# A hybrid RWKV-7 and RG-LRU layer on one core: both roundings of a weight tile ahead of both subtractions

## The chip, the cores and the metric

The kernel runs on one core of a Trainium2 chip. A core has five engines that work side by side, each through its own queue in order: TensorE (PE in the profile; its weight loads are the row PEld), VectorE (DVE), ScalarE (ACT), GpSimd (POOL) and SyncE (SP), which here only issues transfers. The metric is the device time of one execution in microseconds. An engine that reaches an instruction whose input isn't there waits, and everything behind it in its queue waits too.

## The reference, cut to what matters

One layer of a decoder takes 1024 tokens of a prompt and 8 sequences of 4 new tokens, 1056 columns together, each of 1024 channels, all in fp32:

```python
z = x @ w_in                                  # 1024 -> 3*1024+256 RWKV, 2*1024 LRU, 2*1024 gates
yA, S = _rwkv7_branch(z[..., :RWKV_COLS], ...)   # token shift, low-rank decay/gate, wkv state
yB, new_conv, h_last = _rglru_branch(xb, gb, ...)  # conv of 4, gated linear recurrence
merged = sigmoid(ga) * yA + sigmoid(gb2) * yB
h1 = layer_norm(ALPHA * x + merged @ w_o)
y  = layer_norm(ALPHA * h1 + (silu(h1 @ w_ffn_gate) * (h1 @ w_ffn_up)) @ w_ffn_down)
```

The RWKV branch is, for each head of 64 channels, a state S (64 x 64) that each token decays, corrects by a rank-one term and extends by another:

```python
sa = einsum('bhij,bhj->bhi', S, -kk_t)
S = S * w_t + sa * (kk_t * a_t) + v_t * k_t
y_t = einsum('bhij,bhj->bhi', S, r_t)
```

## The kernel before, in words

**Products in three parts.** TensorE multiplies in a rounded fp32 format. To keep the precision, each factor is split into a rounded part and the rest (x into xh and xl, a weight tile into wh and wl), and each product is three matmuls: wh with xh, wh with xl, wl with xh.

**Stages.** First the projection w_in: 58 tiles of 128 output columns, each for two halves of the tokens (one of them in two pieces of 300 and 256 columns, the other in one of 512). A list, STREAM, sets the order in which these tiles come. Eight *units* (half p of the tokens, pair of head groups) of the RWKV branch run beside it as background tasks: the preparation of the operands (rge, kta, arm, rb, bk), the inverse of a triangular block (btmp and bt on VectorE, then bounced through a buffer in memory, scrZ, to zt and tdv), a chain of eight chunks (xs, su), and the gating, whose result mgd goes to memory. The LRU branch and the sample tokens are background tasks too. Then follow the output projection w_o (16 tiles, split again from mgd), the layer norm, the feed-forward part in five splits of its hidden tiles (the long plain stretch of the profile), and the second layer norm.

**Who sets the order.** All instructions go through a `Ticker`, a list scheduler that works while the program is written. Each task is a generator that queues its instructions; only the first pending one of each task is a candidate. The ticker issues the candidate that can start first by its own table of costs, and between equals the one of the task with the smaller priority number. So within a task the order is fixed; between tasks it is decided by these costs. Main-program instructions are recorded at line 246, all instructions of background tasks at line 316, so that nearly all the units' work has the one line L316, and the names of tiles tell it apart.

**Weights.** The class `Weights` runs a task of priority 0 that brings the weight tiles, in order of use, through two raw buffers (wraw, 512 KB each transfer, issued by GpSimd's queue) and two pairs of split buffers (wh, wl). For tile j it waits until tile j − 2 is in use no more, then treats the two halves of the tile (PARTS = 2; `k` holds four of eight blocks of 128 x 128 each): `A` is ScalarE's copy with rounding into wh, `TT` VectorE's subtraction raw − wh into wl. From tile 132 on (N_IN; behind the projection's and LRU's tiles) the second half's subtraction is `PTT`, the same on GpSimd. Then the tile counts as arrived, and the transfer of tile j + 2 is issued into the raw buffer.

Of the kernel before, what the change touches and what calls it, by code (L numbers as in the profile page):

```python
# [345 lines left out]
def tile_hybrid_step(ctx: ExitStack, tc: tile.TileContext, I, O):  # L346
# [16 lines left out]
    def A(out, in_, func=AF.Copy, scale=1.0, bias=0.0):  # L363
        return act.activation(out, in_, func, bias=bias, scale=scale)
# [47 lines left out]
    class Weights:  # L412
# [21 lines left out]
        def split(self):  # L434
            for j, (_, nk) in enumerate(self.srcs):
                while not self.rest if j >= len(self.srcs) - 8 else self.used + len(self.h) <= j:
                    yield
                raw, (h, l) = self.raw[j % len(self.raw)], self.parts(j)
                for part in range(self.PARTS):
                    k = slice(part * nk // self.PARTS, (part + 1) * nk // self.PARTS)  # L440
                    A(h[:, k], raw[:, k])
                    (PTT if part in ON_POOL and j >= N_IN else TT)(l[:, k], raw[:, k], h[:, k].bitcast(F32), OP.subtract)
                tk.later(self.arrived)
                if j + len(self.raw) < len(self.srcs):
                    self.load(j + len(self.raw))
# [32 lines left out]
    with ExitStack() as zctx:  # L478
# [1097 lines left out]
        def merged_first():  # L1576
            for k in range(8):
                split(early[k % 4], k, 544, "mA")
                if k < 4:
                    load_cols(early[k], mgd[k + 4], cols)  # L1580
            yield
# [9 lines left out]
        def merged_last():  # L1591
            t = yield from temps.take()
            stage = [t, pp, vzs[0][:, 0], vzs[0][:, 1]]
            for k in range(8):
                while (6, "fin") not in F or k > 5 and (7, "fin") not in F:
                    yield
                load_cols(stage[k % 4], mgd[k], ((512, 1024),))
                if k > 2:
                    split(stage[(k - 3) % 4], k - 3, 512, "mB")
                if k == 5:  # L1600
                    for x in (3, 4, 5):
                        split(stage[x % 4], x, 512, "mB")
            for x in (6, 7):
                split(stage[x % 4], x, 512, "mB")
# [356 lines left out]
```

## Time and profile before

| | |
|---|---|
| time, median of 3 runs | 2149.74 us |
| the three runs | 2144.78, 2149.74, 2162.22 us |
| the profiled execution, its own time | 2161.04 us |
| its span in the trace | 2159.3 us |
| mean granted clock of TensorE in it | 0.965 |
| TensorE busy | 2057.3 us, 95% |
| VectorE busy | 1239.0 us, 57% |
| ScalarE busy | 1072.5 us, 50% |
| GpSimd busy | 395.7 us, 18% |
| VectorE's subtractions into wl | 344, 263.2 us |
| ScalarE's roundings into wh | 424, 250.7 us |

The profiled execution took 11.3 us longer than the median. Durations and waits come from its trace; a forecast from them is put on the median by its difference. A row of a group gives line, engine, operation, out<-in, the count, busy time and mean, and then the engine's idle time just ahead of these instructions with what ended most of it. A row of the timeline gives start, duration and, in brackets, the idle time ahead with its releaser.

### The profile page before, as it was taken

What the parts mean: (1) busy time and instruction counts of PE and PEld (TensorE: products, weight loads), DVE (VectorE), ACT (ScalarE), POOL (GpSimd) and SP (SyncE); (2) the same over time, 40 slices, a digit from 0 to 9 for tenths busy, and PEclk for the clock granted to TensorE, in tenths of its full rate; (3) what the DMA queues carried; (4) which work ended last, traced back from release to release, by engine and by line L of the source; (5) the groups of instructions that cost most, each with busy time, mean ns of one, the idle gap of its engine ahead of it and who ended that gap; (6) DMA issues with size and microseconds to landing.
All of it is one profiled execution on the core that took longest, in us unless ns stands there. A gap on an engine that the chain in (4) does not pass through costs nothing.

```text
span 2159.3 us, 44129 instructions
## 1 busy us (share of the span) xinstructions
PE 2057.3 (95%) x17664; PEld 1782.9 (83%) x17664; DVE 1239.0 (57%) x2999; ACT 1072.5 (50%) x2491; POOL 395.7 (18%) x813
## 2 busy tenths in 40 slices
PE   7799999989989999999999899999999999999996
PEld 7788888988987777777777697889999999999986
DVE  5576786786777786877867656522322323223227
ACT  4656665757657768676676736821121121121221
POOL 1101211211311310202112020211211111112124
PEclk9899997999999999999989799999999999999998
DMA  4131231231232231222313423211111111112112
GB/s 136 56 97 40 73 102 35 67 87 60 90 112 65 77 94 50 81 72 78 89 45 95 132 96 119 98 55 37 56 49 31 58 45 35 59 35 65 39 40 81
DMA packets 125565, 152.85 MB, mean 71 GB/s; under 512 B 82912, under 2 KB 87424, under 8 KB 125360
## 3 DMA queue, kind: packets, MB, share of 16 engines
q0 software_dynamic: 32576, 112.75, 15.6%
q1 hardware_dynamic: 92784, 37.28, 7.0%
q8 instruction: 139, 2.28, 0.4%
q14 instruction: 66, 0.54, 0.1%
HBM read 132.45 MB, written 17.57 MB: 69 GB/s over the span
## 4 chain that ended last, share of the span: by engine, by line
PE 74%; DVE 11%; ACT 9%; issue 3%; DMA 1%; POOL 1%; POOLq 0%; SPq 0%; DVEq 0%; ACTq 0%
PE bank L246 60%; PE bank L316 15%; DVE tmp L316 2%; ACT tmp L316 2%; DVE wl L316 1%; ACT wh L316 1%; DVE su L316 1%; ACT L316 1%; ACT nz L316 1%; DVE btmp L316 1%; ACT arm L316 1%; DVE bt L316 1%; ACT bk L316 1%; DVE arm L316 1%; DVE rge L316 1%
## 5 line engine op out<-in xcount | busy, mean ns | idle before, releaser
L246 PE MATMUL bank<-xx,wh 128*128 128x512 f32 (+4 forms) x3168 | 801.0, 340 | 28.6 <-ACT xx L246 9.1
L246 PEld LDWEIGHTS bank<-xx,wh 128*128 128x128 f32 x3168 | 547.3, 194 | 89.8 <-ACT xx L246 9.0
L246 PE MATMUL bank<-xx,wl 128*128 128x512 f32 (+4 forms) x1584 | 537.1, 339 | 0.0
L316 DVE TENSOR_TENSOR wl<-wraw,wh 128x512 fp32r<-128x512 f32 (+1 forms) x344 | 263.2, 767 | 265.3 <-ACT wh L316 260.8
L316 ACT ACTIVATE wh<-wraw 128x512 fp32r<-128x512 f32 (+2 forms) x424 | 250.7, 599 | 287.1 <-PE bank L246 248.0
L246 PE MATMUL bank<-hl,wh 128*128 128x272 f32 (+1 forms) x1056 | 342.4, 324 | 0.9 <-DVE hl L316 0.9
L246 PE MATMUL bank<-hh,wh 128*128 128x272 f32 (+1 forms) x1056 | 341.0, 323 | 0.5 <-ACT hh L316 0.5
L246 PE MATMUL bank<-hh,wl 128*128 128x272 f32 (+1 forms) x1056 | 341.3, 323 | 0.0
L246 PEld LDWEIGHTS bank<-xx,wl 128*128 128x128 f32 x1584 | 307.2, 194 | 28.2 <-issue 3.0
L246 PEld LDWEIGHTS bank<-hh,wh 128*128 128x128 f32 x1056 | 198.6, 188 | 17.3 <-ACT hh L316 1.2
L246 PEld LDWEIGHTS bank<-hl,wh 128*128 128x128 f32 x1056 | 198.6, 188 | 17.2 <-DVE hl L316 1.5
L246 PEld LDWEIGHTS bank<-hh,wl 128*128 128x128 f32 x1056 | 198.5, 188 | 15.4
L316 POOL DMA_DIRECT2D wraw<-in_win x114 | 61.9, 543 | 778.4 <-DVE wl L316 480.7
L246 PE MATMUL bank<-u,wh 128*128 128x272 f32 (+1 forms) x864 | 197.5, 322 | 0.0
L316 POOL TENSOR_TENSOR wl<-wraw,wh 128x512 fp32r<-128x512 f32 (+2 forms) x80 | 90.5, 1131 | 525.6 <-ACT wh L316 502.8
L246 PEld LDWEIGHTS bank<-u,wh 128*128 128x128 f32 x864 | 143.9, 188 | 12.9
L316 DVE TENSOR_TENSOR acc<-acc,bank 128x272 f32<-128x272 f32 (+3 forms) x120 | 62.2, 519 | 140.7 <-PE bank L246 138.9
L246 PE MATMUL bank<-u,wl 128*128 128x272 f32 (+1 forms) x432 | 139.4, 323 | 0.0
L316 ACT ACTIVATE sg<-bank 128x272 f32<-128x272 f32 (+1 forms) x66 | 30.8, 466 | 195.8 <-PE bank L246 195.8
L316 DVE TENSOR_TENSOR sg<-sg,bank 128x272 f32<-128x272 f32 (+1 forms) x66 | 34.4, 521 | 157.5 <-PE bank L246 157.4
L316 ACT ACTIVATE u<-sg 128x272 fp32r<-128x272 f32 (+1 forms) x66 | 33.1, 502 | 114.2 <-DVE sg L316 114.2
L316 ACT ACTIVATE su<-bank 64x256 f32<-64x256 f32 (+1 forms) x192 | 60.2, 337 | 59.3 <-PE bank L316 57.0
(248 smaller groups left out, 3154.5 us busy)
## 6 DMA issues: line engine op xcount, KB each, us to landing
wraw<-in_win POOLq DMA_DIRECT2D x116, 512.0 KB, 3.6
wraw<-in_wgu POOLq DMA_DIRECT2D x48, 512.0 KB, 3.5
wraw<-in_wo POOLq DMA_DIRECT2D x16, 512.0 KB, 3.6
wraw<-in_wdn POOLq DMA_DIRECT2D x24, 256.0 KB, 2.9
wraw<-in_wdn POOLq DMA_DIRECT2D x16, 320.0 KB, 3.1
mgd<-yb POOLq DMA_DIRECT2D x32, 128.0 KB, 2.6
out_y<-tmp SPq DMA_DIRECT2D x8, 512.0 KB
scrN<-nz SPq DMA_DIRECT2D x64, 32.0 KB
```

Of the source, the lines that this page charges most:

```text
L246: fn(*args, **kw)
L316: fn(*args, **kw)
```

## The change

Within a weight tile's task the two halves are no longer treated one after the other (rounding, subtraction, rounding, subtraction), but the two roundings are queued first and then the two subtractions. Number, size and engine of the instructions stay.

```diff
-                for part in range(self.PARTS):
-                    k = slice(part * nk // self.PARTS, (part + 1) * nk // self.PARTS)
+                ks = [slice(part * nk // self.PARTS, (part + 1) * nk // self.PARTS) for part in range(self.PARTS)]
+                for k in ks:
                     A(h[:, k], raw[:, k])
+                for part, k in enumerate(ks):
                     (PTT if part in ON_POOL and j >= N_IN else TT)(l[:, k], raw[:, k], h[:, k].bitcast(F32), OP.subtract)
```

Since only a task's first pending instruction is a candidate, the first subtraction can now be issued only after the second rounding. All the ticker's later decisions follow from that, and the order on every engine differs from there on. In the program before, two subtractions into the same wl stand in direct succession on VectorE in 23 places, after the change in 128; two roundings in succession on ScalarE in 75 and 126.

On ScalarE at the opening of the program (the second weight tile, wraw1; lora is the first small weight of the low-rank parts, tmp its raw tile just loaded), before:

```order
L316 ACTIVATE wh1_78<-wraw1_76 128x512
L316 ACTIVATE lora0_121<-tmp_86 64x256
L316 ACTIVATE wh1_78<-wraw1_76 128x512
L316 ACTIVATE lora0_121<-tmp_86 64x256
L316 ACTIVATE tmp_86<-tmp_86 128x8
```

and on VectorE at the same place, before (dv are small vectors derived from parameters):

```order
L316 TENSOR_SCALAR dv_93<-vec_92 128x8
L316 TENSOR_TENSOR wl1_80<-wraw1_76,wh1_78 128x512
L316 TENSOR_SCALAR dv_93<-vec_92 128x8
L316 TENSOR_TENSOR lora1_122<-tmp_86,lora0_121 64x256
L316 TENSOR_TENSOR wl1_80<-wraw1_76,wh1_78 128x512
L316 TENSOR_SCALAR dv_93<-vec_92 128x8
L316 TENSOR_TENSOR lora1_122<-tmp_86,lora0_121 64x256
L316 TENSOR_SCALAR dv_93<-vec_92 128x8 x5
L316 TENSOR_SCALAR tmp_86<-vec_92 128x8
```

The same stretch of VectorE after the change:

```order
L316 TENSOR_SCALAR dv_93<-vec_92 128x8 x3
L316 TENSOR_TENSOR wl1_80<-wraw1_76,wh1_78 128x512 x2
L316 TENSOR_SCALAR dv_93<-vec_92 128x8 x2
L316 TENSOR_TENSOR lora1_122<-tmp_86,lora0_121 64x256
L316 TENSOR_SCALAR dv_93<-vec_92 128x8
L316 TENSOR_TENSOR lora1_122<-tmp_86,lora0_121 64x256
L316 TENSOR_SCALAR dv_93<-vec_92 128x8 x2
L316 TENSOR_SCALAR tmp_86<-vec_92 128x8
```

Both subtractions now stand ahead of both lora subtractions; on ScalarE, likewise, both roundings stand ahead of both lora roundings.

On VectorE in the preparation of the first unit (about 72 us; kta, rge and tmp are its operands), before:

```order
L316 SCALAR_TENSOR_TENSOR tmp_86<-rge0_197,vec_92,tmp_86 128x548
L316 TENSOR_TENSOR wl1_80<-wraw1_76,wh1_78 128x512
L316 SCALAR_TENSOR_TENSOR kta0_198<-kta0_198,dv_93,pp_128 128x512
L316 TENSOR_TENSOR rge0_197<-rge0_197,pp_128 128x512
L316 TENSOR_TENSOR wl1_80<-wraw1_76,wh1_78 128x512
L316 SCALAR_TENSOR_TENSOR kta0_198<-kta0_198,dv_93,pp_128 128x32
```

and after:

```order
L316 SCALAR_TENSOR_TENSOR tmp_86<-rge0_197,vec_92,tmp_86 128x548
L316 TENSOR_TENSOR wl1_80<-wraw1_76,wh1_78 128x512 x2
L316 SCALAR_TENSOR_TENSOR kta0_198<-kta0_198,dv_93,pp_128 128x512
L316 TENSOR_TENSOR rge0_197<-rge0_197,pp_128 128x512
L316 SCALAR_TENSOR_TENSOR kta0_198<-kta0_198,dv_93,pp_128 128x32
```

The long kta and rge steps stood between the two subtractions and now stand behind both. ScalarE has the two roundings of this tile in succession in both programs.

On VectorE at the inverse of unit 3 (about 637 us), around the block steps that lead to zt, before:

```order
L316 TENSOR_TENSOR wl1_80<-wraw1_76,wh1_78 128x512
L316 TENSOR_TENSOR arm_129<-bank3_68,cst_74 64x4x128
L316 TENSOR_TENSOR rb_131<-bank3_68,cst_74 64x4x64
L316 TENSOR_TENSOR wl1_80<-wraw1_76,wh1_78 128x512
L316 TENSOR_TENSOR bn_140<-bn_140,n2_1_146 64x256
L316 TENSOR_TENSOR btmp_142<-bn_140,bt_141 64x15
```

and the end of the stretch after the change:

```order
L316 SCALAR_TENSOR_TENSOR rge0_197<-tmp_86,rge0_197 128x548
L316 TENSOR_TENSOR wl1_80<-wraw1_76,wh1_78 128x512 x2
L316 TENSOR_TENSOR btmp_142<-bn_140,bt_141 64x39
L316 TENSOR_TENSOR bt_141<-bt_141,btmp_142 64x13x3
L316 TENSOR_TENSOR btmp_142<-bn_140,bt_141 64x48
L316 TENSOR_TENSOR bt_141<-bt_141,btmp_142 64x12x4
```

Before, arm, rb and bn of the next group stood between and right behind the two subtractions, and the block steps btmp and bt began after them. After the change the first block steps stand ahead of the pair, and the later ones (from 64x39 on) behind it.

## The prediction

> **What bounds the kernel now.** I read the page's head and busy shares first, then the chain that ended last, then the two groups of the weight split.
>
> ```profile
> span 2159.3 us, 44129 instructions
> PE 2057.3 (95%) x17664; PEld 1782.9 (83%) x17664; DVE 1239.0 (57%) x2999; ACT 1072.5 (50%) x2491; POOL 395.7 (18%) x813
> PE 74%; DVE 11%; ACT 9%; issue 3%; DMA 1%; POOL 1%; POOLq 0%; SPq 0%; DVEq 0%; ACTq 0%
> L316 DVE TENSOR_TENSOR wl<-wraw,wh 128x512 fp32r<-128x512 f32 (+1 forms) x344 | 263.2, 767 | 265.3 <-ACT wh L316 260.8
> L316 ACT ACTIVATE wh<-wraw 128x512 fp32r<-128x512 f32 (+2 forms) x424 | 250.7, 599 | 287.1 <-PE bank L246 248.0
> ```
>
> TensorE is busy 95% of the span and holds 74% of the chain; it is idle for 2159.3 − 2057.3 = 102 us in all. That is the most that any better order of the other engines can save in idle time. The two groups below it look tempting: VectorE is idle 265.3 us ahead of its subtractions, 260.8 of them for the rounding. But the releaser of the rounding is TensorE (248.0 us): the split runs as far ahead as its two buffers let it, and then waits for TensorE to finish with a tile. Most of this waiting is slack. The stages tell where it is not (columns: window, its length, then the busy time with the count for PE, PEld, DVE, ACT and POOL, then granted clock, DMA share, GB/s).
>
> ```profile
> 23.00:1390.00 1367.00, 1300.15 (x12990) 1098.74 (x12991) 989.36 (x2558) 902.94 (x2144) 228.93 (x612) 0.95 0.27 80
> 1390.00:2107.00 717.00, 716.30 (x4370) 645.10 (x4369) 197.60 (x313) 150.19 (x305) 135.45 (x164) 1.00 0.15 47
> 1392.85 714.12 PE bank L246 x4359
> ```
>
> From 1390 to 2107 us TensorE is busy 716.30 of 717.00 us at full clock, and the chain of waits there is one piece of 4359 matmuls. No order of roundings and subtractions can gain there, and with VectorE at 198 us and ScalarE at 150 of 717 nothing is near being late. Whatever the change does, it does before 1390 us, in the projection with the recurrent units beside it: there TensorE is idle 66.85 us (1367.00 − 1300.15), VectorE busy 72% and ScalarE 66%.
>
> Next, the waits: who waits for a split weight (after the name: us in all, count, mean)?
>
> ```profile
> DVE wl L316 <- ACT wh L316: 54.9, 62, 3.5
> ACT wh L316 <- PE bank L246: 33.5, 26, 4.5
> PE bank L316 <- DVE zt L316: 13.7, 6, 3.7
> PE bank L316 <- DMA zt<-scrZ: 6.5, 3, 4.5
> PE bank L316 <- DVE su L316: 8.1, 13, 1.5
> PE bank L246 <- DVE tmp L316: 5.3, 1, 5.3
> ```
>
> The first two rows are those of 23 to 1390 us, the others TensorE's waits over the whole run. None of TensorE's waits is for a wh or a wl: the weights are never late. It waits for the units' own steps (zt, su, tmp), which share VectorE's in-order queue with the subtractions. So **the change can act only through what stands behind a subtraction on VectorE, or behind a rounding on ScalarE.** It is the same arithmetic by the same instructions, with no transfer more or less.
>
> **The change part by part.** A weight tile's task offers only its first pending instruction. Before, a first subtraction could be issued while the second rounding was still pending; now it follows the second rounding in issue order, and the two subtractions mostly stand back to back on VectorE (23 places before, 128 now). A subtraction here takes 0.69 us. From 54.9 us of VectorE waiting inside its queue, some goes: by the time the first of a pair comes up, its rounding is older. Against that, whatever stood between the halves now stands behind both.
>
> *The opening.* The timeline, columns start, duration, engine, operation, idle before:
>
> ```profile
> 15.78 0.62 ACT L316 ACTIVATE wh<-wraw 128x512 fp32r<-128x512 f32 x1
> 18.53 0.42 ACT L316 ACTIVATE lora<-tmp 64x256 fp32r<-64x256 f32 x1 [2.13 <-DMA tmp<-in_lora]
> 18.85 0.61 ACT L316 ACTIVATE wh<-wraw 128x512 fp32r<-128x512 f32 x1
> 19.50 0.69 DVE L316 TENSOR_TENSOR wl<-wraw,wh 128x512 fp32r<-128x512 f32 x1
> 20.28 0.42 DVE L316 TENSOR_TENSOR lora<-tmp,lora 64x256 fp32r<-64x256 f32 x1
> 20.72 0.46 DVE L316 TENSOR_SCALAR dv<-vec 128x8 f32<-128x8 f32 x5
> 23.03 0.84 PE L246 MATMUL bank<-xx,wh 128*128 128x300 f32 x2 [5.31 <-DVE tmp L316]
> ```
>
> The second rounding stands behind a rounding that waits 2.13 us for a transfer. Its subtraction (0.69 us at 19.50) then delays the second lora subtraction and the tmp steps, for which TensorE idles 5.31 us. Now both roundings run ahead of that wait (from 15.78), both subtractions use VectorE's idle time, and of the dv steps two in place of five come after the last lora subtraction. The second lora rounding then follows the first directly (18.95 to 19.4), and its subtraction starts at about 19.5 in place of 20.28; 3 × 0.09 us of dv (0.46 for five) go too: **−1.0 us**. What is late next is the same tmp chain.
>
> *The first unit.*
>
> ```profile
> 72.85 0.63 ACT L316 ACTIVATE wh<-wraw 128x512 fp32r<-128x512 f32 x1 [0.77 <-PE bank L246]
> 72.11 0.69 DVE L316 TENSOR_TENSOR wl<-wraw,wh 128x512 fp32r<-128x512 f32 x1 [0.45 <-ACT wh L316]
> 72.72 0.75 DVE L316 SCALAR_TENSOR_TENSOR kta<-kta,dv,pp 128x512 f32<-128x512 f32 x1
> 73.38 0.68 DVE L316 TENSOR_TENSOR rge<-rge,pp 128x512 f32<-128x512 f32 x1
> 73.98 0.69 DVE L316 TENSOR_TENSOR wl<-wraw,wh 128x512 fp32r<-128x512 f32 x1
> 74.85 0.72 DVE L316 TENSOR_TENSOR tmp<-tmp,kta 128x548 f32<-128x548 f32 x1
> 76.39 3.42 PE L316 MATMUL bank<-arm,bk 64*128 64x128 f32 x16 [3.46 <-ACT arm L316]
> ```
>
> Here the second rounding waits for TensorE until 72.85 and ends at 73.48. kta and rge fill that hole on VectorE. Now both subtractions come first, so the second one starts at about 73.5 and ends at 74.2; kta and rge follow it (0.75 and 0.68, less overlaps of about 0.1), and tmp starts at about 75.65 in place of 74.85: **+0.8 us** if nothing else gives way. From −0.75 (the hole would have closed anyway) to +1.4 (both subtractions in the way) is what the rows allow.
>
> *Unit 3.* VectorE makes zt, on which TensorE waits longest of this kind.
>
> ```profile
> 637.06 0.69 DVE L316 TENSOR_TENSOR wl<-wraw,wh 128x512 fp32r<-128x512 f32 x1
> 641.46 0.29 DVE L316 TENSOR_TENSOR zt<-zt,bank 128x128 f32<-128x128 f32 x1
> 641.80 1.06 PE L316 MATMUL bank<-tdv,nz 32*32 32x32 f32 x32 [3.67 <-DVE zt L316]
> 642.80 0.80 PE L246 MATMUL bank<-xx,wl 128*128 128x512 f32 x1
> 636.58 0.40 PE L246 MATMUL bank<-xx,wl 128*128 128x512 f32 x1
> ```
>
> After the change the pair and some ten pairs of btmp and bt steps stand ahead of zt, and six matmuls in place of ten cover the wait. That is four matmuls of 0.40 us less cover, **+1.6 us** at most, or nothing where zt also comes earlier; the whole stall gone would be −3.67. I take 0, since the inverse's own steps were only shifted past a burst that stands in both.
>
> The chip's clock is in these rows: the same matmul takes 0.40 us before the stall and 0.80 behind it. [...]
>
> *All other tiles before 1390 us.* What 1 us on VectorE is worth there: its chain share is 11% of 2159.3, or 237 us, of 989.36 us busy, so 0.24 of each. VectorE's waits for a rounding, 54.9 us, are worth 54.9 × 0.24 = 13 us. They could all go (−13) or double (+13). A first subtraction like that at 72.11 waits right behind its own rounding; in a pair it comes up a rounding later, and only the second can still wait. Half of the halves, less what the second ones wait longer, as at 72.85: I choose a third as gone, **−4 us**.
>
> *ScalarE.* Its own 33.5 us of waits for TensorE put whatever stands behind the second rounding late; a pair of roundings holds that queue 0.6 us longer (599 ns in the group's row). The pairs grow from 75 to 126, so 51 × 0.6 × 9/50 (its chain share, 9%, by its busy share, 50%) = +5.5 us at the upper end, and nothing at the lower end, as the second rounding mostly followed soon anyway. I take 0 and keep 5.5.
>
> Sum: −1.0 + 0.8 + 0 − 4 + 0 = about **−4 us** against the profiled execution's 2161.04 us (span 2159.3), so 2157. That execution is 11.3 us above the median 2149.74; put on the median, **2146 us**.
>
> **The rivals.**
>
> [...] The order changes everywhere before 1390 us, and the first unit's gaps may close.
>
> ```profile
> 54.00:108.00 54.00, 42.99 (x299) 40.63 (x298) 32.06 (x79) 34.78 (x94) 8.30 (x26) 0.81 0.19 56
> 85.58 2.04 PE L316 MATMUL bank<-arm,bk 64*128 64x128 f32 x12 [4.16 <-DVE rb L316]
> 90.48 0.84 PE L246 MATMUL bank<-xx,wh 128*128 128x300 f32 x2 [2.86 <-DVE rge L316]
> ```
>
> Three gaps (3.46, 4.16, 2.86) make 10.5 us, and the window's clock is 0.81: 54 × (0.95 − 0.81)/0.95 = 8 us. With VectorE's waits of 13 us gone as well: −31, or **2119**. For it: the gaps name VectorE and ScalarE, and only order delays them. Against it: VectorE's order around 72 us moves the wrong way.
>
> *Slower, pairs block the chain.* The place is VectorE in the units: 105 more pairs, each of which holds the queue 0.69 us longer for the step behind it, which the first subtraction alone would have let pass. 105 × 0.69 × 0.24 = 17 us. Idle TensorE also costs clock: in the window above 11.0 us of idle time (54.00 − 42.99) went with 8 us lost to the clock, so 0.73 us more for each: 17 × 1.73 = +30, or **2180**. It decides from the point at which units' steps stand behind more than half of the pairs on a path to TensorE; the stalls named for zt and su (13.7 + 8.1 us) would then about double. Against it: TensorE's queue has projection matmuls ready between the units' steps, which cover 0.7 us.
>
> *It only shuffles.* Tiles' roundings that were issued together already (75 pairs on ScalarE) and slack elsewhere make the sum zero: **2150**. For it: no wait of TensorE names a weight. Against it: nearly all rows between 23 and 1390 us move.
>
> **How the numbers follow.** The forecast, with its own range 2133 to 2159 (the ±13 us around its place), gets 0.45; only shuffled 0.20; faster 0.16; slower 0.19. Within 1% of 2149.74 is 2128 to 2171, about what a measurement of this kernel can tell from no change. All of the shuffle and nearly all of the forecast lie inside; of the faster rival 0.14 is beyond it, of the slower one 0.15, and the forecast adds 0.03 and 0.01: faster 0.17, same 0.67, slower 0.16. The range reaches down to the faster rival's 2119 less its place's own few us, and up to the slower one's 2180.
>
> **What would show it.** Right: TensorE's restart near 22.0 in place of 23.03; tmp behind the pair near 75.6 in the first unit, with the gap of 3.46 about 0.8 longer; VectorE's wait for wh before 1390 us near 37 us in place of 54.9; still one unbroken piece of some 4350 matmuls in the feed-forward part; no wait of TensorE that names wl or wh. Wrong: TensorE's busy time changed by more than the clock explains, waits named zt or su grown by 10 us or more (the slower rival), or a granted clock in the first 108 us near that of the rest (the faster one). The forecast rests most on the 0.24 per us of VectorE's time, a mean over a stage whose stalls are few and local; one stall more or less at a unit's inverse is 4 us, and the whole forecast.

## The result, and the profile after

The changed kernel takes 2180.07 us (median of 4 runs, 2172.97 to 2185.53) against 2154.05 us before (4 runs): a ratio of 1.0117, 95% interval 1.0089 to 1.0145. It is slower by 26 us, where 4 us faster was forecast. Its profiled execution has a span of 2177.3 us, 18.0 more than that of before, which was taken some 7 us above the median of its kernel. The ratios in this document are the record's estimates over runs taken side by side, and need not be the quotient of two medians. The page's head and the two groups of the weight split:

```profile
span 2177.3 us, 44101 instructions
PE 2067.5 (95%) x17664; PEld 1785.4 (82%) x17664; DVE 1234.5 (57%) x2999; ACT 1074.3 (49%) x2491; POOL 393.5 (18%) x813
L316 ACT ACTIVATE wh<-wraw 128x512 fp32r<-128x512 f32 (+2 forms) x424 | 246.0, 599 | 294.8 <-PE bank L246 273.4
L316 DVE TENSOR_TENSOR wl<-wraw,wh 128x512 fp32r<-128x512 f32 (+1 forms) x344 | 252.8, 762 | 240.0 <-ACT wh L316 239.0
```

The work is the same, by count and by length. TensorE's idle time is 2177.3 − 2067.5 = 109.8 us in place of 102.0, and its busy time is 10.2 us longer for the same 17664 matmuls. Where is the loss? The chain's long piece and the two stages, as windows:

```profile
1406.53 718.46 PE bank L246 x4371
23.00:1404.00 1381.00, 1305.88 (x12982) 1096.99 (x12980) 983.77 (x2552) 900.63 (x2136) 226.43 (x612) 0.95 0.27 79
1404.00:2125.00 721.00, 718.97 (x4374) 647.50 (x4375) 197.85 (x314) 153.76 (x310) 135.74 (x164) 1.00 0.15 47
```

The feed-forward piece ends at 1406.53 + 718.46 = 2124.99 us, before at 1392.85 + 714.12 = 2106.97: 18.0 us later, the whole difference. Behind it nothing changes, and in it next to nothing: here the piece takes in 12 matmuls more at its start. The first matmul of the feed-forward part (on hh) starts at 1372.0 us in place of 1356.4, so 15.6 of the 18.0 us are lost ahead of that part, and the rest at its start. TensorE's waits over the whole run and VectorE's for wh (window 23 to 1390 us), in the order us in all, count, longest:

```profile
PE bank L316 <- ACT tmp L316: 11.6, 7, 3.0
PE bank L316 <- DVE tmp L316: 11.1, 8, 3.8
PE bank L316 <- DVE zt L316: 8.6, 6, 2.8
PE bank L316 <- DVE su L316: 7.8, 15, 1.5
PE bank L316 <- DMA zt<-scrZ: 0.3, 1, 0.3
PE bank L246 <- ACT wh L316: 1.9, 1, 1.9
PE bank L246 <- DVE wl L316: 1.1, 1, 1.1
DVE wl L316 <- ACT wh L316: 31.9, 27, 6.5
```

The last column is the longest single wait; the prediction called it a mean, but no sum of it used that column. Before, the first two of these were small:

```profile
PE bank L316 <- DVE tmp L316: 5.0, 3, 3.6
PE bank L316 <- ACT tmp L316: 2.4, 3, 1.0
```

The stalls that the prediction watched shrank (zt 13.7 to 8.6, its transfer 6.5 to 0.3), others took their place (tmp by ScalarE +9.2, by VectorE +6.1), and for the first time matmuls wait for a weight tile (wh or wl), 3.0 us in all. VectorE's wait for the rounding fell from 54.9 to 31.9 us, and TensorE's idle time grew all the same.

One of the new stalls, at 339 us. ScalarE's timeline, and TensorE's row behind it (start, duration, in brackets the idle time ahead):

```profile
338.50 1.15 ACT L316 ACTIVATE wh<-wraw 128x512 fp32r<-128x512 f32 x2
339.54 0.76 ACT L316 ACTIVATE su<-bank 64x256 f32<-64x256 f32 x2
340.31 0.38 ACT L316 ACTIVATE bkt<-bank 128x256 f32<-128x256 f32 x1
340.70 0.90 ACT L316 ACTIVATE tmp<-bank 32x64 f32<-32x64 f32 x4
341.66 0.56 PE L316 MATMUL bank<-tmp 64*64 64x64 f32 x6 [2.22 <-ACT tmp L316]
```

A pair of roundings stands ahead of three steps of the units, and TensorE waits 2.22 us for the last of them. It looks like the rival of the blocking pairs. Whether pairs make the loss is what the experiments had to tell.

**The clock.** TensorE's granted clock goes with a part of it. Each run lists its own: the changed kernel's four are 2172.97 us at 0.967, 2179.15 and 2180.98 at 0.963, 2185.53 at 0.960; the kernel before, in one series on one chip, ran from 2148.84 us at 0.972 to 2172.51 at 0.959, with 2155.43 and 2156.04 at 0.967. At the equal clock of 0.967 the change costs about 17 us, by one run against two. A straight line through 89 runs of before in the experiments' series (a 90th, marked slow on record, is left out) falls by 1.6 us for each 0.001 of clock. The changed kernel's four runs lie 19 us above that line on the mean, and the remaining 6 us or so go with their lower clock (0.963 on the mean, against 0.967).

### The profile page after: what moved, and what is told of

The parts are those of the page before. It is cut to its first block, busy times and chain, and to the rows that moved or that the text cites. A ratio compares the mean times of both kernels' runs of the same rounds, so it can differ in the third digit from the quotient of the medians.

```text
span 2177.3 us, 44101 instructions
## 1 busy us (share of the span) xinstructions
PE 2067.5 (95%) x17664; PEld 1785.4 (82%) x17664; DVE 1234.5 (57%) x2999; ACT 1074.3 (49%) x2491; POOL 393.5 (18%) x813
## 3 DMA queue, kind: packets, MB, share of 16 engines
q0 software_dynamic: 32576, 112.75, 15.6%
## 4 chain that ended last, share of the span: by engine, by line
PE 54%; DVE 6%; ACT 3%; issue 1%; DMA 0%; SPq 0%; POOL 0%; POOLq 0%; DVEq 0%; ACTq 0%
PE bank L246 47%; PE bank L316 6%; DVE tmp L316 1%; DVE wl L316 1%; DVE st L316 1%; DVE su L316 1%; ACT L316 1%; ACT tmp L316 0%; ACT wh L316 0%; ACT su L316 0%; DVE btmp L316 0%; DVE bt L316 0%; ACT nz L316 0%; DVE yb L316 0%; DVE ag L316 0%
## 5 line engine op out<-in xcount | busy, mean ns | idle before, releaser
L246 PE MATMUL bank<-xx,wh 128*128 128x512 f32 (+4 forms) x3168 | 809.3, 341 | 31.0 <-ACT xx L246 9.0
L316 ACT ACTIVATE wh<-wraw 128x512 fp32r<-128x512 f32 (+2 forms) x424 | 246.0, 599 | 294.8 <-PE bank L246 273.4
L316 DVE TENSOR_TENSOR wl<-wraw,wh 128x512 fp32r<-128x512 f32 (+1 forms) x344 | 252.8, 762 | 240.0 <-ACT wh L316 239.0
L316 ACT ACTIVATE su<-bank 64x256 f32<-64x256 f32 (+1 forms) x192 | 60.4, 338 | 67.7 <-PE bank L316 65.7
L246 PEld LDWEIGHTS bank<-u,wl 128*128 128x128 f32 x432 | 81.2, 188 | 6.1
```

Of the source, the lines that this page charges most:

```text
L246: fn(*args, **kw)
L316: fn(*args, **kw)
```

## The experiments

Two theories. **A, pairs:** paired roundings and subtractions hold up what stands behind them. **B, plan:** the rule makes the ticker place all other work anew, and this new order is worse; the pairs themselves hardly matter. Later B was parted: B1, the order of before is an unusually good one, and nearly any other costs; B2, the changed rule makes worse orders.

All ratios are to the kernel before, run on the same chip at the same time, with 95% intervals.

### Pairs on an unchanged plan, and the new plan without paired subtractions

The ticker plans as before (or as after), but an instruction can be given out in another's place. TensorE's order then stays that of before (or of after): in the traces, all but 8 or fewer of the 17664 matmul rows stand in the same place.

```diff
+    def emit_with(self, *moves):
+        # (i, j): the i-th of the instructions just queued is given out in the j-th's place
...
                     A(h[:, k], raw[:, k])
                     TT(l[:, k], raw[:, k], ...)
+                tk.emit_with((-2, -4), (-3, -1))   # pairs: second rounding with the first, first subtraction with the second
```

> The plan of before is kept: TensorE's order is that of before to the last row, and all other work stands where it stood. Only the four instructions of a weight tile are moved into pairs: the second rounding goes out right behind the first, the first subtraction right ahead of the second. Theory A (the pairs themselves hold up what stands behind them on VectorE and ScalarE): most of the 26 us come back, 2170 to 2180. Theory B (the pairs are harmless, the loss is in the new plan, that is in where the ticker puts all the other work once the rule is changed): within 5 us of before, 2145 to 2160, with VectorE's wait for wh before 1390 us cut from 55 to about 35 us.

Measured: 2165.37 us, 1.0042 (1.0019 to 1.0064). That lies between the two ranges, in neither. The run also forms more pairs than the change does: of the 132 tiles ahead of the feed-forward part, the traces have both roundings in direct succession for 10 before, 54 after the change and all 132 here; both subtractions for 23, 128 and 132.

> The reverse: the plan of the changed kernel is kept, TensorE's order to the last row, but each first subtraction goes out right behind the second rounding's place and no two subtractions or roundings are planned as a pair any more. Theory A (pairs hold up the units): most of the loss goes, 2150 to 2160. Theory B (the plan): it stays, 2172 to 2185.

Measured: 2178.11 us, 1.0101 (1.0082 to 1.0120). That is in theory B's range. One thing in the expectation was put wrongly: only the subtractions are taken apart (39 of the 132 still stand in succession); the 126 pairs of roundings stay. The stall shown above stays too, where the pair of roundings still stands:

```profile
335.49 0.63 ACT L328 ACTIVATE wh<-wraw 128x512 fp32r<-128x512 f32 x1
336.00 0.63 ACT L256 ACTIVATE wh<-wraw 128x512 fp32r<-128x512 f32 x1
338.64 0.56 PE L328 MATMUL bank<-tmp 64*64 64x64 f32 x6 [2.38 <-ACT tmp L328]
```

So pairs forced on the unchanged plan cost 9 to 15 us (with the second measurement below), with many more pairs of roundings than the change makes; how much of the change's 26 us its own pairs make isn't shown. Taking the subtractions' pairs out of the new plan brings back nothing beyond the intervals. Theory A isn't enough. The same run shows what VectorE's waits for the rounding are worth. With the subtractions apart they are 61.2 + 4.3 = 65.5 us (the first and the second subtraction now have lines of their own), 33.6 us more than in the changed kernel, and the kernel isn't slower for it:

```profile
DVE wl L256 <- ACT wh L328: 61.2, 42, 6.5
DVE wl L328 <- ACT wh L256: 4.3, 7, 1.1
```

### By engine, and on another plan

```diff
+                tk.emit_with((-2, -4))             # roundings in pairs alone
...
+                tk.emit_with((-3, -1))             # subtractions in pairs alone
```

> Plan of before; only the second rounding goes out right behind the first, the subtractions stay where they were. If the pairs' price is on ScalarE (what stands behind the first rounding waits 0.6 us longer, at 2 in 3 of the tiles), 5 to 9 us slower than before, 1.003 to 1.005 of it. If it is on VectorE, no difference or a gain of some us, since the second subtraction never waits for its rounding: 0.996 to 1.001.

> Plan of before; only the first subtraction is held back to the second one's place, the roundings stay. If the price is on VectorE, 5 to 9 us slower (1.003 to 1.005): whatever stood between the halves still does so, but what is behind the second subtraction waits 0.69 us longer. If it is on ScalarE, within 2 us of before.

Measured: roundings alone 0.9972 (0.9949 to 0.9996), subtractions alone 1.0001 (0.9973 to 1.0028). Neither costs anything that can be told from no change, and the subtractions alone (132 pairs) are nearly those of the change (128). Since both together had cost 0.4%, roundings alone and both ran again side by side, in five rounds:

> Paired roundings alone on the plan of before. If they are a gain: 0.995 to 0.998 of before, its interval below 1. If that was chance (the rule on the feed-forward part alone, which leaves all ahead of it, came out at 0.998): 0.998 to 1.001.

> Both pairs on the plan of before. If they cost together what neither costs alone: 1.003 to 1.006, with its interval above that of the paired roundings. If the first result was a chip's: 0.997 to 1.001, the product of the two single ones.

Measured: 0.9988 (0.9961 to 1.0016), and 1.0068 (1.0046 to 1.0089). The small gain was chance or below what can be told; the loss of both together holds, a little above the expected range, with its interval above that of the paired roundings. A part of it shows in the trace as idle time of TensorE: the windows from 23 us to the first matmul of the feed-forward part (on hh), of before, of the paired roundings, of both pairs:

```profile
23.00:1356.00 1333.00, 1266.89 (x12727) 1066.29 (x12728) 967.51 (x2511) 871.34 (x2074) 221.47 (x604) 0.95 0.27 80
...
23.00:1343.00 1320.00, 1260.32 (x12727) 1061.04 (x12727) 966.54 (x2508) 869.97 (x2071) 220.59 (x604) 0.96 0.27 80
...
23.00:1362.00 1339.00, 1267.54 (x12730) 1065.08 (x12731) 965.04 (x2511) 870.49 (x2075) 217.37 (x604) 0.95 0.26 79
```

1333.00 − 1266.89 = 66.1 us idle before, 59.7 with paired roundings, 71.5 with both (74.0 in the first run of both, 67.7 with paired subtractions alone). That is 5 to 8 us more than before; the rest of the 9 to 15 us isn't traced to a place. VectorE's waits for wh don't follow the time: 54.9 us before, then, in this order, with paired roundings, with paired subtractions alone, and least of all in the slowest of these kernels, with both pairs:

```profile
DVE wl L328 <- ACT wh L256: 37.4, 39, 4.5
...
DVE wl L258 <- ACT wh L328: 33.2, 38, 2.5
...
DVE wl L258 <- ACT wh L256: 11.7, 10, 3.6
```

Why two moves that cost nothing cost 9 to 15 us together isn't settled: what stands on VectorE is the same as with paired subtractions alone, what stands on ScalarE as with paired roundings alone. The clock doesn't settle it: against the line through the runs of before, paired roundings lie 2 us below it, paired subtractions 4 us above, and both 12 us above. Two more runs asked whether this price holds on another plan (the random part of 10 ns is explained below):

> The old rule's plan with seed 3 (1.0059 of before) and pairs on both engines on it. If pairs cost what they cost on the plan of before (0.42%), 1.009 to 1.012. If that price was only the loss of a picked interleaving, within 0.2% of 1.0059.

> The changed rule's plan with seed 3 (1.0157 of before), with each first subtraction given out at the second rounding's place. If pairs cost 0.4% on any plan, 1.010 to 1.013. If the plan carries the time, as with the changed kernel (1.0101 against 1.0117), 1.013 to 1.018.

Measured: 1.0133 (1.0101 to 1.0164) against 1.0059 without the pairs: +0.7%, above the expected range and near the second measurement on the plan of before. And 1.0171 (1.0139 to 1.0204) against 1.0157: again nothing comes back. Pairs on both engines cost 0.4 to 0.7% where they are forced on a plan that was made without them; in a plan that was made with them, taking the subtractions apart gains nothing. What taking the roundings apart there would gain was not run.

### Other plans of the same rule

Now the rule stays, and the ticker's estimates get a random part that means nothing on the chip.

```diff
-            end = at + self.FIXED[e] + self.cost(e, f, out, ins, args, kw)
+            end = at + self.FIXED[e] + self.cost(e, f, out, ins, args, kw) + self.rnd.uniform(-0.01, 0.01)
```

> The rule of before; only the planner's own estimate of each instruction's length gets a random part of at most 10 ns (seed 1), which means nothing on the chip but gives another plan. By its placing of the units' steps this plan stands nearer to that of the changed kernel than to that of before. Theory B1 (the plan of before is a lucky one, and any other costs): 2165 to 2185, as the changed kernel. Theory B2 (the rule itself makes worse plans): within 8 us of before, 2146 to 2162.

> As with seed 1, seed 2: this plan stands nearer to that of before. Theory B1: slower than before by 10 us or more, 2165 to 2185. Theory B2: 2146 to 2162.

> The old rule, an unpicked seed (3). B1: 2165 to 2185. B2: 2146 to 2162.

> The changed rule with the same random part (seed 1). Theory B1: the same spread as the old rule with random parts, 2160 to 2185, so that the two rules can't be told apart. Theory B2: near the changed kernel, 2172 to 2188, clear of the old rule's.

> As before, seed 2. Theory B1: 2160 to 2185, mixed with the old rule's. Theory B2: 2172 to 2188.

> The changed rule, the same unpicked seed. B1: within the spread of the old rule's unpicked plans, or up to 10 us above, 2165 to 2195. B2: over 2180, clear of all of the old rule's.

| random part | old rule | changed rule |
|---|---|---|
| none | 1 | 1.0117 (1.0089 to 1.0145) |
| seed 1 | 1.0136 (1.0096 to 1.0176) | 1.0173 (1.0133 to 1.0212) |
| seed 2 | 1.0077 (1.0054 to 1.0101) | 1.0049 (1.0022 to 1.0076) |
| seed 3 | 1.0059 (1.0037 to 1.0082) | 1.0157 (1.0120 to 1.0194) |

This is the result that settles most. Ten nanoseconds on the planner's estimates, with the old rule, cost 0.6 to 1.4%. The changed rule's plans lie between 0.5 and 1.7%. The means of the three seeds are 1.0091 and 1.0126; their difference, 0.35%, is smaller than the spread of either column, so that the two rules can't be told apart by it. In times, the old rule's seeds took 2182.70, 2172.95 and 2164.24 us: the first two in B1's range, the third just below it, and none in B2's. The changed rule's took 2192.34, 2165.60 and 2184.81: the first above both ranges, the second in B1's alone, the third in both. **B1 holds as far as three plans can show it:** the plan of before is better than each of the old rule's other plans that ran, and the changed rule's loss is of the size of theirs. B2 as it was put fails; a smaller part of the rule's own isn't excluded. The windows of both kernels with seed 1, old rule first, and that of the changed kernel last:

```profile
23.00:1379.00 1356.00, 1273.41 (x12731) 1065.93 (x12732) 964.68 (x2511) 874.71 (x2076) 217.50 (x604) 0.95 0.26 78
...
23.00:1383.00 1360.00, 1271.71 (x12726) 1067.78 (x12724) 961.28 (x2506) 872.58 (x2072) 210.75 (x604) 0.95 0.26 78
...
23.00:1372.00 1349.00, 1274.36 (x12726) 1065.97 (x12725) 961.86 (x2506) 871.64 (x2072) 218.64 (x604) 0.95 0.26 79
```

VectorE, ScalarE and GpSimd are busy as long as ever; TensorE's idle time is 82.6, 88.3 and 74.6 us, against 66.1 before.

The clock of each run tells more on the rules. Measured from the line through the runs of before, which takes the clock out, the old rule's three seeds and the picked plan below lie 23, 16, 11 and 15 us above it, and the changed rule's five plans (none, the three seeds, picked) 19, 24, 10, 19 and 12 us: 16 and 17 on the mean. What is left between the rules is in the granted clock, 0.966 on the mean of the old rule's plans and 0.961 of the changed rule's (0.959 to 0.966, plan by plan). Why the changed rule's plans were granted less isn't shown.

### Plans picked by the ticker's own account

> The changed rule with the random part of at most 10 ns, and of eleven seeds the one (5) whose end the ticker's own account puts first. If the loss is that of a plan that was not picked (B1), a picked plan of the new rule gets most of it back, 2155 to 2168. If the rule itself makes the loss (B2), it stays at 2172 to 2188.

> The same for the old rule (of twelve seeds number 6). B1: 2152 to 2165, near before, clear of the unpicked ones (2173 and 2183). If the ticker's account says nothing on the chip's time, it lies with those, 2165 to 2185.

Measured: changed rule 2179.56 us, 1.0125 (1.0090 to 1.0159), old rule 2170.71 us, 1.0081 (1.0056 to 1.0105); in the second one the first output, y of the prompt, comes out changed, so that it is read for its time alone. Both expectations of B1 failed: picking a plan by the planner's own account got nothing back, and the changed rule's picked plan lies in the range that was given for B2. The old rule's lies with its unpicked plans, as was expected if that account says nothing on the chip's time. So the changed rule's result doesn't speak for B2: picking didn't help the old rule either.

### The rule by itself, and two tasks

> The changed rule for tiles from 132 on alone (the feed-forward part); all ahead of it is as before. Both theories: no difference, 2150 to 2158, the feed-forward part's chain again one piece of some 4360 matmuls and 714 us. A loss of over 5 us would mean that the subtractions on GpSimd are held up by the second rounding.

```diff
+                both = j >= N_IN
+                for part, k in enumerate(ks):
+                    A(h[:, k], raw[:, k])
+                    if not both:
+                        TT(l[:, k], ...)
...
```

Measured: 2154.12 us, 0.998 (0.996 to 1.000). Its chain has the feed-forward piece of before, 714.12 us:

```profile
1376.76 714.12 PE bank L246 x4359
23.00:1341.00 1318.00, 1252.20 (x12730) 1053.89 (x12730) 968.39 (x2509) 870.80 (x2073) 220.83 (x604) 0.96 0.27 81
```

With the rule in the feed-forward part nothing is lost. It is a weak test of pairs: the second subtraction is on GpSimd there, and in the trace the two roundings stood in direct succession in 71 of the 80 tiles before, and do in all 80 now.

> Roundings and subtractions are two tasks, so that neither holds back the other: a first subtraction may go out before or after the second rounding, whichever can start first. Theory A: pairs fall from 128 to 77 on VectorE, about half of the loss stays, 2160 to 2170. Theory B: a third plan, whose time says nothing on pairs; anywhere from 2145 to 2185. If the freedom itself is worth something, it is below before, 2135 to 2145.

```diff
                     A(h[:, k], raw[:, k])
+                    tk.later(self.round)
...
+        def subtract(self):
+            for j, (_, nk) in enumerate(self.srcs):
+                for part in range(self.PARTS):
+                    while self.rounded <= j * self.PARTS + part:
+                        yield
...
```

Measured: 2166.55 us, 1.0047 (1.0029 to 1.0066). That is in the ranges of both theories, so it doesn't decide between them; what was hoped of the freedom itself didn't come. It is again a plan worse than before.

No version beat the kernel before by more than can be told from no change.

## Why the prediction was wrong, step by step

- **What bounds the kernel: right.** The feed-forward part's long piece wasn't touched, all of the loss lies before 1407 us.
- **"The change can act only through what stands behind a subtraction on VectorE, or behind a rounding on ScalarE": the step that failed most.** The sum priced the places where the moved instructions stand, and put the new order of all other work at nothing. The prediction itself says, in its faster rival, that the order changes everywhere before 1390 us; no term of its sum, and no bound of its range of ±13 us, holds a price for that. With the new order kept and the subtractions apart, the loss stays (1.0101). New orders of the old rule cost 0.6 to 1.4%, 13 to 29 us, without the changed rule.
- **The opening, −1.0 us: right.** TensorE restarts at 21.91 (22.0 was forecast), with the gap down from 5.31 to 3.80:

```profile
17.11 1.28 DVE L316 TENSOR_TENSOR wl<-wraw,wh 128x512 fp32r<-128x512 f32 x2
19.38 0.42 DVE L316 TENSOR_TENSOR lora<-tmp,lora 64x256 fp32r<-64x256 f32 x1
21.91 0.84 PE L246 MATMUL bank<-xx,wh 128*128 128x300 f32 x2 [3.80 <-DVE tmp L316]
```

- **The first unit, +0.8 us: wrong.** VectorE did nearly what was forecast, tmp came 3.3 us after the first subtraction in place of 2.7. But TensorE's gap is 3.46 us as before: it waits for ScalarE's arm, and tmp is not on that path.

```profile
70.71 0.69 DVE L316 TENSOR_TENSOR wl<-wraw,wh 128x512 fp32r<-128x512 f32 x1
74.04 0.72 DVE L316 TENSOR_TENSOR tmp<-tmp,kta 128x548 f32<-128x548 f32 x1
74.75 0.71 PE L316 MATMUL bank<-arm,bk 64*128 64x128 f32 x4 [3.46 <-ACT arm L316]
```

- **Unit 3, 0 us: wrong, and the wrong question.** The stall of 3.67 us for this unit's zt is 1.05 us after the change. Over all units the stalls for zt and its transfer fell by 11.3 us; those for tmp alone grew by 15.3. A list of stalls that exist says nothing of those that a new order makes.
- **All other tiles, −4 us: the term of the sum that failed.** VectorE's waits for wh went as told (37 us forecast, 31.9 measured), but the price did not: 0.24 us for each of VectorE's, taken from the chain's shares, would have made 23 us of waits 5.5 us of gain. (It also divides VectorE's chain share of the whole span by its busy time in one window.) On the unchanged plan, the paired subtractions took these waits down to 33.2 us and the paired roundings to 37.4, and neither gained anything that can be told (1.0001, 0.9988); both pairs took them down to 11.7 and cost 0.7%. On the new plan 33.6 us more of them cost nothing. So these waits were slack.
- **ScalarE, 0 us: right by itself**, as the paired roundings alone show; with paired subtractions beside them, on the plan of before, 9 to 15 us that no step had.
- **The rival "it only shuffles", 2150 us: its place was wrong.** It took a shuffle for a draw around the old time. On the chip it is a draw around about 1.009 of it (the mean of the old rule's three seeds), because the old order is better than each of these. Some 20 us (0.9% of 2154) on the mean of those three are the price of a new plan; that these and the pairs' 9 to 15 add up was not shown.
- **The rival of the blocking pairs** named the time, 2180, by another way, so that its hit is luck: zt and su were to double, and went from 13.7 to 8.6 and from 8.1 to 7.8 us, and the subtractions' pairs, which it priced, cost nothing alone that can be told (1.0001). Its 0.73 us of clock for each us of idle time, and the faster rival's 8 us of clock, were the author's estimates from one window, 54 to 108 us, and no run shows that the clock follows the idle time there. After the change this window has more idle time (54.00 − 41.53 = 12.47 us, and 11.01 before) at a higher clock (0.84, and 0.81 before):

```profile
54.00:108.00 54.00, 41.53 (x302) 39.20 (x302) 31.36 (x80) 34.17 (x92) 7.19 (x20) 0.84 0.19 56
```

- **The signs.** Of the forecast's signs of being right, the restart, tmp on VectorE and VectorE's waits came; the first unit's gap didn't grow, and two waits of TensorE name a weight.

What stays open is why pairs on both engines cost what neither costs alone, what the change's own pairs cost, why the changed rule's plans were granted a lower clock, and why this one order is so good; the new stalls of the changed kernel are many and short (15 for tmp, none over 3.8 us), not one place.

## What to carry to other kernels

In a kernel whose order a list scheduler makes, a change of one task's order is a change of the whole order: before its own effect is priced, make a few neutral changes of plan (here 10 ns on the estimates) and see what they cost, since the kernel at hand may stand at the good end of that spread, as this one did. To see the change alone, hold the plan and move only the instructions. And a wait inside the queue of an engine that isn't the bottleneck was worth nothing here; give it a price only where a trace shows the bottleneck waiting for what stands behind it.

## What the runs showed of the hardware

Two programs that are the same up to the feed-forward part ran at unequal clocks there, and took unequal times. The kernel with the rule in the feed-forward part alone and the kernel before have the same idle time of TensorE up to that part (1318.00 − 1252.20 = 65.8 us, and 66.1), but TensorE is busy 1252.20 and 1266.89 us for it, at a granted clock of 0.96 and 0.95 in these windows, and a mean over the span of 0.973 and 0.965. That is 14.7 us, more than half of the effect in question, and the profiled execution of before, 2161.04 us at 0.965, lies above its kernel's median of 2154.05. The clock also differs from run to run of one program: the kernel before ran, in one series, from 2148.84 us at 0.972 to 2172.51 at 0.959, a range of 1.1%.

It changes within one execution too. In the profiled one of before, around the stall of 3.67 us in unit 3, and at a place with no such stall just ahead:

```profile
634.00:640.00 6.00, 3.72 (x106) 2.94 (x106) 5.58 (x16) 0.00 (x0) 0.53 (x1) 1.00 0.15 40
642.00:648.00 6.00, 6.00 (x74) 4.64 (x71) 5.56 (x20) 2.88 (x6) 0.00 (x0) 0.50 0.01 3
...
318.00:324.00 6.00, 5.95 (x142) 4.85 (x142) 1.28 (x4) 5.73 (x16) 0.00 (x0) 1.00 0.39 127
324.00:330.00 6.00, 6.00 (x77) 5.25 (x76) 2.12 (x10) 2.98 (x6) 0.00 (x0) 0.50 0.00 0
```

Behind that stall the granted clock was 0.50 in place of 1.00, and it was 0.50 from 324 us as well, where TensorE had been busy for 5.95 of the 6 us ahead. What sets it isn't shown.
